# A row softmax streamed through SBUF: sixteen tiles of eight rows in six buffers become twelve tiles of eight, twelve and four rows in four buffers

## The chip, the core and the metric

The kernel runs on one NeuronCore of one Trainium2 chip. The metric is the time of one execution on the device, in microseconds (us). Five executions of the kernel before took 317.83 to 318.44 us, with a median of 317.9 us. A profile was taken of one further execution; all clock readings below are us from the first instruction of that execution.

## What is computed

The input `x` is 32 x 512 x 1024 in float32, so 16,384 rows of 1024 numbers, 67.11 MB. Each row is divided by a temperature of 0.5 and goes through a softmax.

```python
scaled = x / temperature
shifted = scaled - np.max(scaled, axis=-1, keepdims=True)
exp_x = np.exp(shifted)
return (exp_x / np.sum(exp_x, axis=-1, keepdims=True)).astype(np.float32)
```

The output is as large as the input. So 67.11 MB must be read from HBM and 67.11 MB written back; each row is read once and written once.

## The kernel before

A tile holds 128 x k rows: each of the 128 SBUF partitions holds k consecutive rows of the matrix, 4 KiB each. Below, "rows" always means rows per partition, so the whole job is 128 rows and one row is 128 x 4 KiB = 0.524 MB. `TILES` (L10) lists the tiles: sixteen of eight rows. Loads, arithmetic and stores all use the same buffer; `BUFS` (L11) says how many buffers there are, six of 32 KiB per partition.

`load` (L57 to L62) takes the next tile of the list and issues its load on the SP queue (L61). In DRAM, the eight rows of one partition lie side by side (`dram`, L50 to L53), so a tile is moved as 128 contiguous pieces of 32 KiB. A load into a buffer that was used before waits until the store out of that buffer has landed.

The arithmetic runs over groups of `GROUP` = 4 rows (L13, list built in L39 to L48), so a tile of eight rows has two groups. For a group g there are four steps:

- `maximum` (L64): VectorE (DVE) finds the row maxima, one TENSOR_REDUCE over 128 x 4096 numbers (L70), and multiplies them by -2 to a bias (L73). The first group of a tile needs the whole tile to have landed, as the load is one DMA.
- `exponential` (L75): ScalarE (ACT) runs one ACTIVATE for each row (L79), which also adds up the row's sum.
- `divide` (L88): DVE takes the reciprocal of the sums (L91) and multiplies each row by it (L93).
- `store` (L97): after the last group of a tile, the store of the whole tile is issued on the ACT queue (L101), and then `load` is called, which gives SP the load that reuses this buffer.

The order on every engine is the program order, since the body runs under a manual schedule (L107). The loop at L110 interleaves neighbouring groups: for each g it issues `maximum(g)` and `exponential(g)`, and after them `divide(g - 1)` and `store(g - 1)`. So DVE works on the maxima of group g while ACT still has the exponentials of g - 1. It also means that the store of a tile comes after the first `maximum` of the next tile, which waits for the next tile's load.

Of the kernel before, what the change touches and what calls it, by code (L numbers as in the profile page):

```python
# [1 line left out]

# [4 lines left out]

TILES = [[8]] * 16  # L10
BUFS = 6  # L11

GROUP = 4  # L13


@with_exitstack
def kernel(
    ctx: ExitStack,
    tc: tile.TileContext,
    x: bass.AP,  # L20
    temperature: bass.AP,
    out: bass.AP,
):
    nc = tc.nc
    f32 = mybir.dt.float32
    scale = 1.0 / float(temperature)
    extreme = mybir.AluOpType.max if scale > 0 else mybir.AluOpType.min

    P = 128
    xf = x.flatten_outer_dims()  # L30
    of = out.flatten_outer_dims()
    n, d = xf.shape
    assert sum(sum(ks) for ks in TILES) * P == n

    data = ctx.enter_context(tc.tile_pool(name="data", bufs=BUFS))
    stats = ctx.enter_context(tc.tile_pool(name="stats", bufs=4))


    groups, first, r = [], [], 0  # L39
    for i, ks in enumerate(TILES):  # L40
        first.append(r)
        r += sum(ks)
        a = 0
        for k in ks:
            for b in range(0, k, GROUP):
                m = min(GROUP, k - b)
                groups.append((i, a + b, m, (a, k) if b + m == k else None))
            a += k  # L48

    def dram(t, i):  # L50
        k = sum(TILES[i])
        block = t[P * first[i] : P * (first[i] + k), :]
        return block.rearrange("(p k) d -> p k d", p=P, k=k)  # L53

    tiles, small = [], []

    def load():  # L57
        i = len(tiles)
        if i < len(TILES):
            xt = data.tile([P, sum(TILES[i]), d], f32, name="xt")  # L60
            nc.sync.dma_start(out=xt, in_=dram(xf, i))  # L61
            tiles.append(xt)  # L62

    def maximum(g):  # L64
        i, a, k, _ = groups[g]
        top, bias, sums, recip = (
            stats.tile([P, k], f32, name=name) for name in ("top", "bias", "sums", "recip")
        )
        small.append((bias, sums, recip))
        nc.vector.tensor_reduce(  # L70
            out=top, in_=tiles[i][:, a : a + k, :], axis=mybir.AxisListType.X, op=extreme
        )
        nc.vector.tensor_scalar_mul(bias, in0=top, scalar1=-scale)  # L73

    def exponential(g):  # L75
        i, a, k, _ = groups[g]
        bias, sums, _ = small[g]
        for b in range(k):
            nc.scalar.activation(  # L79
                tiles[i][:, a + b, :],  # L80
                tiles[i][:, a + b, :],
                mybir.ActivationFunctionType.Exp,
                bias=bias[:, b : b + 1],
                scale=scale,
                accum_out=sums[:, b : b + 1],
            )

    def divide(g):  # L88
        i, a, k, _ = groups[g]
        _, sums, recip = small[g]  # L90
        nc.vector.reciprocal(recip, sums)  # L91
        for b in range(k):
            nc.vector.tensor_scalar_mul(  # L93
                tiles[i][:, a + b, :], in0=tiles[i][:, a + b, :], scalar1=recip[:, b : b + 1]
            )

    def store(g):  # L97
        i, _, _, part = groups[g]
        if part:
            a, k = part  # L100
            nc.scalar.dma_start(out=dram(of, i)[:, a : a + k, :], in_=tiles[i][:, a : a + k, :])  # L101
            if a + k == sum(TILES[i]):
                load()

    with tc.manual_schedule():  # L107
        for _ in range(BUFS):
            load()
        for g in range(len(groups) + 1):  # L110
            if g < len(groups):
                maximum(g)
                exponential(g)
            if g > 0:
                divide(g - 1)
                store(g - 1)


# [1 line left out]
_INS = ['x', 'temperature']  # L120
_OUTS = [((32, 512, 1024), 'float32')]

_NUMBERS = {'temperature': 0.5}


# [26 lines left out]
```

## Time and profile before

| What | Value |
|---|---|
| median of five executions | 317.9 us |
| the profiled execution: its own time | 317.9 us |
| the profiled execution: span from first to last instruction | 316.0 us |
| time around the span (the difference) | 1.9 us |
| DVE busy | 235.5 us, 75% of the span |
| ACT busy | 149.6 us, 47% of the span |
| bytes moved by the 16 DMA engines | 134.25 MB, 425 GB/s over the span |
| loads: number, size, median from issue to landing | 16, 4096 KB, 50.2 us |
| stores: number, size, median from issue to landing | 16, 4096 KB, 38.7 us |

How to read the views used below. The page cuts the span into 40 slices; a digit is the busy share of a slice in tenths, for DMA the mean over the core's 16 DMA engines. For a DMA queue, the page gives its packets, the MB it moved, and the time that its packets took as a share of the span of all 16 engines. q1 carries the loads from SP, q10 the stores from ACT, q14 fetches instructions. The same view can be asked for any stretch of the span; there a packet counts with its whole duration in the stretch in which it starts, so that a short stretch can show more than 100%. A row of the groups gives line, engine, operation, shapes and count, then the busy time in us and the mean ns of one, then the engine's idle time ahead of it and what ended most of it.

### The profile page before, as it was taken

The numbers are of one execution on the slowest core, as the hardware profiler recorded it, in microseconds if no ns is written. First come the engines' busy times: TensorE is split into PE (matmuls) and PEld (weight loads), VectorE is DVE, ScalarE is ACT, GpSimd is POOL, SyncE is SP. The second block draws the span as 40 slices with busy tenths as digits, with TensorE's granted clock in tenths as the row PEclk, the third lists the DMA queues.
The fourth block names the chain that finished last, engine by engine and source line by source line (L and its number), as shares of the span: only waits on it lengthen the run. The fifth ranks groups of instructions, "written<-read, shape, count | busy, mean of one in ns | idle before, by whom it ended". The sixth has DMA issues, their size and how long they took to land.

```text
span 316.0 us, 620 instructions
## 1 busy us (share of the span) xinstructions
DVE 235.5 (75%) x224; ACT 149.6 (47%) x257; POOL 0.2 (0%) x4
## 2 busy tenths in 40 slices
DVE  0399999999689494994949859498693976949720
ACT  0176666666526255361554605546064560645500
POOL 0000000000000000000000000000000000000000
DMA  8999999999999999999999999999999999999996
GB/s 332 406 456 419 377 460 402 460 417 444 423 440 435 431 440 427 448 415 448 415 452 411 452 407 456 411 456 415 448 423 441 435 427 440 423 448 415 452 411 274
DMA packets 4612, 134.25 MB, mean 425 GB/s; under 512 B 512, under 2 KB 512, under 8 KB 512
## 3 DMA queue, kind: packets, MB, share of 16 engines
q1 hardware_dynamic: 2304, 67.11, 49.7%
q10 hardware_dynamic: 2304, 67.11, 49.2%
q14 instruction: 4, 0.03, 0.0%
HBM read 67.11 MB, written 67.11 MB: 425 GB/s over the span
## 4 chain that ended last, share of the span: by engine, by line
DVE 49%; DMA 32%; another core or an unknown queue 9%; ACT 5%; issue 1%; DVEq 0%; SPq 0%
DVE top L70 29%; DMA xt<-in_x_dram 20%; DVE xt L93 18%; DMA out_dram<-xt 12%; ACT xt L79 5%; DVE recip L91 1%; DVE bias L73 1%; DVEq L147 0%; SPq L61 0%
## 5 line engine op out<-in xcount | busy, mean ns | idle before, releaser
L79 ACT ACTIVATE xt<-xt,bias 128x1024 f32<-128x1024 f32 x128 | 145.4, 1137 | 136.9 <-DVE recip L91 119.5
L70 DVE TENSOR_REDUCE top<-xt 128x4 f32<-128x4096 f32 x32 | 141.3, 4416 | 62.6 <-DMA xt<-in_x_dram 62.6
L93 DVE TENSOR_SCALAR xt<-xt,recip 128x1024 f32<-128x1024 f32 x128 | 87.7, 749 | 1.1
L79 ACT ACTIVATION_READ_ACCUMULATOR xt<-xt,bias 128x1 f32 x128 | 23.8, 186 | 0.0
L79 ACT ACT_TABLE_LOAD x1 | 1.3, 1283 | 13.0 <-DMA xt<-in_x_dram 13.0
L91 DVE RECIPROCAL recip<-sums 128x4 f32<-128x4 f32 x32 | 5.5, 171 | 2.1 <-ACT xt L79 2.1
L73 DVE TENSOR_SCALAR bias<-top 128x4 f32<-128x4 f32 x32 | 5.4, 170 | 1.1
L133 POOL MEMSET const-uint8-127<- 128x1 uint8 x1 | 0.1, 102 | 0.0
L133 POOL MEMSET const-bfloat16-1.0<- 128x1 bf16 x1 | 0.1, 101 | 0.0
L133 POOL MEMSET const-float32-0.0<- 128x1 f32 x1 | 0.1, 98 | 0.2 <-issue 0.2
L133 POOL MEMSET const-float32-1.0<- 128x1 f32 x1 | 0.1, 98 | 0.0
## 6 DMA issues: line engine op xcount, KB each, us to landing
xt<-in_x_dram SPq DMA_DIRECT2D x16, 4096.0 KB, 50.2
out_dram<-xt ACTq DMA_DIRECT2D x16, 4096.0 KB, 38.7
```

The lines of the kernel that those rows point to most:

```text
L70: nc.vector.tensor_reduce(out=top, in_=tiles[i][:, a : a + k, :], axis=mybir.AxisListType.X, op=extreme)
L73: nc.vector.tensor_scalar_mul(bias, in0=top, scalar1=-scale)
L79: nc.scalar.activation(tiles[i][:, a + b, :], tiles[i][:, a + b, :], mybir.ActivationFunctionType.Exp, bias=bias[:, b : b + 1], scale=scal ...
L91: nc.vector.reciprocal(recip, sums)
L93: nc.vector.tensor_scalar_mul(tiles[i][:, a + b, :], in0=tiles[i][:, a + b, :], scalar1=recip[:, b : b + 1])
L133: nc = _bacc.Bacc("TRN2", target_bir_lowering=False, num_devices=1)
```

## The change

The list of tiles becomes one tile of eight rows, nine of twelve, one of eight and one of four: twelve tiles, again 128 rows. There are four buffers, each as large as the largest tile, 48 KiB per partition; four times 48 KiB is the 192 KiB that six times 32 KiB were. A twelve-row tile has three groups, so there are 32 groups as before, and the instructions on DVE and ACT are the same in kind and number. There are 24 DMAs where there were 32.

The loop gets a second order. `alone` is true where group g is the first of a new tile and the tile of g - 1 is the tenth of the list or a later one (index 9 or 10 of 0 to 11). This is so at two places: between the last twelve-row tile and the eight-row tile, and between the eight-row tile and the four-row tile. There, `divide(g - 1)` and `store(g - 1)` come ahead of `maximum(g)` and `exponential(g)` and not after them.

```diff
-TILES = [[8]] * 16
-BUFS = 6
+TILES = [[8]] + [[12]] * 9 + [[8], [4]]
+BUFS = 4
...
         for g in range(len(groups) + 1):
+
+            alone = 0 < g < len(groups) and groups[g][0] > groups[g - 1][0] >= len(TILES) - 3
+            if alone:
+                divide(g - 1)
+                store(g - 1)
             if g < len(groups):
                 maximum(g)
                 exponential(g)
-            if g > 0:
+            if g > 0 and not alone:
                 divide(g - 1)
                 store(g - 1)
```

## The prediction

> **What bounds the kernel now.** I first read slices and queues on the page: is one resource full from end to end?
>
> ```profile
> DMA  8999999999999999999999999999999999999996
> q1 hardware_dynamic: 2304, 67.11, 49.7%
> q10 hardware_dynamic: 2304, 67.11, 49.2%
> ```
>
> The DMA engines are: 98.9% of 316.0 us is 312.5 us of packets, and only the first and the last slice show a hole. Next, whether the engines are also waited for. The waits of all engines say:
>
> ```profile
> ACT xt L79 <- DVE recip L91: 119.5, 25, 7.9
> DVE top L70 <- DMA xt<-in_x_dram: 62.6, 12, 12.9
> ```
>
> DVE sits 62.6 us waiting for loads, so the chain of waits, which puts 49% of the span on DVE, only follows it from load to load. Third, the pace of the full stretch, in the DMA view of 40 to 280:
>
> ```profile
> DMA packets 3557, 103.84 MB, mean 433 GB/s; under 512 B 385, under 2 KB 385, under 8 KB 385
> q1 hardware_dynamic: 1777, 51.91, 50.1%
> q10 hardware_dynamic: 1776, 51.91, 50.1%
> ```
>
> Both queues always have work and share equally. One row (0.524 MB) costs 0.524 / 433 = 1.211 us of all engines, 2.42 us while the two queues share. The kernel ends when 256 row-moves are through, unless at some moment both queues are empty. So the change can gain only in packets, in the start or in the end, and lose only where it makes a hole.
>
> **Packets: the one thing removed.** 4608 data-queue packets less the page's 512 small ones leave 4096 of 32 KiB: 32 DMAs of 128 pieces, 256 for each engine. After: nine tiles x 8 pieces x 2 directions = 144 of 48 KiB, 32 of 32 KiB and 16 of 16 KiB, together 192. 64 fewer; their fixed part is gained. It comes from two sizes. A 32 KiB packet takes 50.1% x 16 x 240 / (51.91 MB / 32 KiB = 1584) = 1.2146 us. Two 8 KB instruction fetches stand in the DMA view of 65.02 to 65.38:
>
> ```profile
> q14 instruction: 2, 0.02, 10.7%
> ```
>
> 10.7% x 16 x 0.36 / 2 = 0.308 us each. Fixed part: (4 x 0.308 - 1.2146) / 3 = 5.8 ns, from 4 to 8 ns with the rounding. 64 x 5.8 ns = **0.37 us gained** (0.24 to 0.54). This is an estimate: a fetch does not end in SBUF, and no packet over 32 KiB was seen. Bounds for the longer packet: none of the gain (0), or it is cut up on the way, 0.5 to 1.3 us lost (below). I take 0.37, as the two sizes seen lie on that side. The 8 small packets fewer on each engine I count at nothing.
>
> The Trainium skill (DMA: Bandwidth & Descriptors, Where 436 GB/s comes from) puts the ceiling at 435.2 GB/s. The row says 433; at the ceiling the 134.2 MB would take 308.4 us for 310.0, so by the page no longer packet could gain more than 1.6 us.
>
> **The start.** Tile 0 is still eight rows, issued first and landed at 12.9: nothing moves. The hole it contains is the latency of the first load, unchanged. There is one loss where the first store joins the loads; q1 in the DMA views of 33.8 to 35.0 and of 35.0 to 37:
>
> ```profile
> q1 hardware_dynamic: 16, 0.52, 130.3%
> ```
> ```profile
> q1 hardware_dynamic: 16, 0.52, 85.3%
> ```
>
> 16 packets, one per engine: 1.303 x 1.2 = 1.56 us and 0.853 x 2.0 = 1.71 us, for 1.21. So 0.35 + 0.49 = 0.84 us is lost once. After, the first store is still a 32 KiB one, among 48 KiB loads. Bounds: all of it saved (-0.84), or half as much again (+0.42). I take no change, since the event is the same.
>
> **The middle: fewer, larger buffers.** The load into a buffer waits for the store out of it, so I check whether the loads run dry. Before: the first store is issued at 32.6, and q10 first moves at 37.2 (no q10 packet in the view of 35.0 to 37), 4.6 us later. By then 8 + (37.2 - 12.9 - 0.84) / 1.211 = 27.4 rows are loaded; this lead stays, as the queues share equally. It foretells the page's medians. After load k+1 lands, store k is issued 7.4 us later (next maximum and divide) and is through (27.4 - 8) x 2.42 = 46.9 us after that landing: 39.5 from issue, the page has 38.7. The load that reuses the buffer lands 5 x 19.37 - 46.9 = 50.0 later; the page has 50.2. Of these 50 us only 19.4 are its own transfer, the rest is waiting in the queue.
>
> After: tile 1 (20 rows in) lands at 12.9 + 12 x 1.211 = 27.4, store 0 is issued at 34.8 and moves at 39.4; the lead is 8 + (39.4 - 12.9 - 0.84) / 1.211 = 29.2 rows. A twelve-row tile takes 29.1 us in each queue. Store k is through (29.2 - 12) x 2.42 = 41.7 us after load k+1 lands; the next load has 3 x 29.1 - 41.7 = 45.5 us, of which it needs 29.1. 16 us remain to spare (31 before). DVE needs 3 x 7.39 = 22.2 us of 29.1. So **no hole, nothing gained or lost**. Were this cover gone, the stores would run alone at the full pace and still no engine would be idle.
>
> **The end: new order, smaller tiles.** Before (timeline, engine line op, start first):
>
> ```profile
> 282.65 4.42 DVE L70 TENSOR_REDUCE top<-xt 128x4 f32<-128x4096 f32 x1 [4.49 <-DMA xt<-in_x_dram]
> ...
> 299.43 0.18 DVE L91 RECIPROCAL recip<-sums 128x4 f32<-128x4 f32 x1 [1.91 <-ACT xt L79]
> 299.64 2.74 DVE L93 TENSOR_SCALAR xt<-xt,recip 128x1024 f32<-128x1024 f32 x4
> 302.42 0.34 ACTq L101 DMA_DIRECT2D out_dram<-xt  x1
> ```
>
> The last load lands at 282.6; 32.6 us of stores remain until the last lands (302.42 + 12.8 = 315.2), and the engines stay full. So the end does not wait for arithmetic now, and a shorter last tile has no wait to remove. It must only keep up. By the lead, loads would end at 37.2 + (128 - 27.4) x 2.42 = 280.9 before (it was 282.6, so I add 1.7) and at 39.4 + 98.8 x 2.42 + 1.7 = 280.4 after; tile 10 lands 9.7 earlier at 270.7, tile 9 at 251.3. SP issues loads 10 and 11 after stores 6 and 7, whose 80 and 92 rows are out at 234.8 and 263.8, in time.
>
> Each step: maximum and bias 4.6, exponentials of a group 4.65, reciprocal and multiply 2.95. Tile 9: three interleaved groups 22.2; then, as its last divide now stands alone, 1.7 of waiting for ACT and 2.95: store 9 at 278.2. It's due when store 8 is out (104 rows, 285.0). Tile 10: 4.6 + 4.4 + 2.95, then 1.9 of waiting and 2.95: store 10 at 295.0, due at 299.5. Tile 11: 4.6 + 4.65 + 2.95: store 11 at 307.2. The two orders written out cost DVE about 3.6 us of waiting that interleaving would hide, beside which the stores of tiles 9 and 10 run; nothing else is queued behind those waits but the next maximum on DVE and its exponentials on ACT. In exchange store 9 passes 4.6 us of maximum, and store 10 no longer waits for load 11. Due time of store 11: the end without a hole is 315.2 - 0.4 = 314.8; its own four rows take 4.8, and before, the last store spent 12.8 - 9.7 = 3.1 us on issue, queue and landing: 306.9. The sum lands on the edge. Without the 1.7 I added it is 1.4 us early, with it 0.3 late; I take **0**, and each us that tile 9 lands later costs one.
>
> A rule that speaks against the small last tile: equal shares by bytes are what the row above shows, for equal packets. The Trainium skill (DMA: Bandwidth & Descriptors, Queues, rings and completion order) says that an engine takes turns between queues by packets, so a load in 16 KiB packets beside stores in 48 KiB ones would get a quarter. By that, load 10 would land some 5 us and load 11 some 14 us later than in my sum, about 276 and 294, still ahead of the DVE times at which they are needed (278 and 295). No run here has shown unequal packets.
>
> **Sum.** 316.0 - 0.37 + 0 = 315.6 us of span, and 1.9 around it: **317.5 us**. The profiled execution's own time is the median, 317.9, so nothing is added. That's 0.1% faster; about 0.2% (0.64 us) is what a measurement of this kernel can tell from no change.
>
> **Rivals.**
>
> - The first-store loss goes as well: 317.5 - 0.8 = 316.7. For it: it falls on two packets per engine only, and other packets are then in flight. Against: the joining store is unchanged.
> - The end runs dry (slower). Place: between stores 10 and 11, DVE being the chain. Point: tile 9 landing after 251. Price: one for one; 2 us later gives 319.5. For it: the sum has no margin. Against: 1.7 of it was added on top of the lead.
> - The pieces are not moved whole: cut in two (24 KiB) an engine has 288 + 32 + 16 = 336 packets, 80 more, +0.5 instead of -0.4: 318.4; cut into 16 KiB, 480, +1.3: 319.2. The change would then not do what it says. Against: 32 KiB pieces move whole. I set 318.8.
>
> **Chances.** Forecast 0.58, with its own range 316.9 to 318.3; first-store loss gone 0.13; end dry 0.14; pieces cut or paced worse 0.15. Faster by over 0.2% (under 317.3): 0.13 and about a quarter of the forecast's 0.58, 0.27. Slower by over 0.2% (above 318.5): 0.14 and two thirds of 0.15, 0.24. Within: 0.49. Range 316.6 to 319.5: it takes in most of the first and third rivals and half of the second.
>
> **What would show it.** Queues with 1728 packets each (24 DMAs for both: 1536 + 192 each), DMA 9 in every slice but first and last, 433 to 435 GB/s in the full stretch, loads about 45 us from issue to landing, last store issued near 305 to 307 with stores full up to it. It's wrong if a slice between 280 and 312 shows a hole, if packets are more, or if the pace falls.

## The result, and the profile after

The changed kernel takes 318.63 us (median of 28 executions, 318.18 to 320.61) against 317.95 us of the kernel before (48 executions): ratio 1.0033, 95% interval 1.0024 to 1.0041. It's **slower by 0.7 us**, where 0.4 us faster was forecast. The time lies in the forecast range (316.6 to 319.5), but the sign is the other one. A second series of the same kernel (e12 below) gave 1.0017 (1.0007 to 1.0027), so the size is 0.2 to 0.3%. The executions of the changed kernel scatter more: 18 of 28 lie from 318.2 to 318.9, six from 320.2 to 320.7. The profiled execution took 318.2 us, 316.4 of them its span, so it is one of the shortest.

Slices and queues on the page of the changed kernel, as they were read for before:

```profile
DMA  8999999999999999999999999999999999999995
...
q1 hardware_dynamic: 1728, 67.11, 49.6%
q10 hardware_dynamic: 1728, 67.11, 49.1%
```

The packets are as many as foretold, 1728 in each queue, and no slice but the first and the last has a hole (a stretch in which engines are idle). The share, 98.7% of 316.4, is 312.3 us of packets (312.5 before). So there is neither more DMA work nor a hole, and still the end is later. The DMA view of 40 to 280 has the old pace; only the shares differ:

```profile
DMA packets 2527, 104.02 MB, mean 433 GB/s; under 512 B 272, under 2 KB 272, under 8 KB 272
q10 hardware_dynamic: 1264, 53.74, 51.7%
q1 hardware_dynamic: 1259, 50.25, 48.5%
```

The arithmetic is not late either. The end in the timeline, as shown for before:

```profile
290.20 4.42 DVE L70 TENSOR_REDUCE top<-xt 128x4 f32<-128x4096 f32 x1
...
299.58 0.18 DVE L91 RECIPROCAL recip<-sums 128x4 f32<-128x4 f32 x1 [4.75 <-ACT xt L79]
299.79 2.74 DVE L93 TENSOR_SCALAR xt<-xt,recip 128x1024 f32<-128x1024 f32 x4
302.56 0.34 ACTq L101 DMA_DIRECT2D out_dram<-xt  x1
```

The last store is issued at 302.56, as before (302.42), though it carries half as much.

What did move is seen only when the 16 DMA engines are counted one by one. Every DMA ends on every engine with one small packet (the page of the changed kernel has 384 for its 24 DMAs); in the last stretch, "under 512 B" is therefore the number of engines that have finished. The DMA views of 312.6 to 313.05, 313.05 to 314.2 and 314.2 to 316.5, first of before:

```profile
DMA packets 1, 0.03 MB, mean 73 GB/s; under 512 B 0, under 2 KB 0, under 8 KB 0
DMA packets 16, 0.07 MB, mean 57 GB/s; under 512 B 14, under 2 KB 14, under 8 KB 14
DMA packets 2, 0.00 MB, mean 0 GB/s; under 512 B 2, under 2 KB 2, under 8 KB 2
```

and of the changed kernel:

```profile
DMA packets 15, 0.10 MB, mean 219 GB/s; under 512 B 9, under 2 KB 9, under 8 KB 9
DMA packets 11, 0.13 MB, mean 114 GB/s; under 512 B 3, under 2 KB 3, under 8 KB 3
DMA packets 7, 0.05 MB, mean 21 GB/s; under 512 B 4, under 2 KB 4, under 8 KB 4
```

By 313.05 nine engines are done where none was: the first ends at 312.70 for 313.09, by the records of the closing packets, which is the gain that was worked out. But four engines, for two, end after 314.2, the last at 315.24 for 314.83. The kernel waits for the last one. From the first engine's end to the last one's it is 1.74 us before and 2.54 us in the changed kernel.

Single packets show what makes an engine late. A window that holds the start of one packet gives its duration, share x 16 x width. DMA views of the changed kernel at 235.8 to 235.9, 236.1 to 236.15, 188.88 to 188.92 and 281.3 to 281.5:

```profile
q14 instruction: 1, 0.01, 19.3%
```
```profile
q1 hardware_dynamic: 1, 0.05, 294.1%
```
```profile
q1 hardware_dynamic: 1, 0.05, 355.0%
```
```profile
q10 hardware_dynamic: 1, 0.05, 77.1%
```

The first is an instruction fetch of 0.31 us; the second the 48 KiB packet behind it, 2.35 us where others take 1.815. One fetch holds one engine back by 0.31 + 0.54 us. The kernel before has these too, four fetches in each trace. The records don't name the engine, but on one engine a packet starts as the one ahead of it ends, so it can be followed from packet to packet. Before, the four fetches fall on two engines, two on each, and these two end last, at 314.49 and 314.83, 1.40 and 1.74 us behind the first; fetches and excess behind them add up to 1.37 and 1.69 us. So it is the fetches that make these two late.

The third (2.27 us) and the fourth (2.47 us) have no fetch near them. The third starts where the load queue has just gone over to its next tile, the fourth beside the 16 KiB packets of the last load. I call a packet slow that takes over 60 ns more than its size needs. After 40 us, before has 4 slow packets, all behind fetches, 1.8 us of excess in all; the changed kernel has 23, 6.5 us in all. Of the 19 behind no fetch, 12 start where a queue has just gone over to its next tile, and all but one fall on the five engines that end last. The very last had no fetch at all.

### The profile page after: what moved, and what is told of

The parts are those of the page before. It is cut to its first block, busy times and chain, and to the rows that moved or that the text cites. A ratio compares the mean times of both kernels' runs of the same rounds, so it can differ in the third digit from the quotient of the medians.

```text
span 316.4 us, 605 instructions
## 1 busy us (share of the span) xinstructions
DVE 235.5 (74%) x224; ACT 149.5 (47%) x257; POOL 0.2 (0%) x4
## 3 DMA queue, kind: packets, MB, share of 16 engines
q1 hardware_dynamic: 1728, 67.11, 49.6%
q10 hardware_dynamic: 1728, 67.11, 49.1%
## 4 chain that ended last, share of the span: by engine, by line
DMA 77%; DVE 12%; ACT 5%; issue 1%; DVEq 0%; SPq 0%; ACTq 0%
DMA xt<-in_x_dram 40%; DMA out_dram<-xt 38%; DVE top L70 8%; ACT xt L79 5%; DVE xt L93 3%; DVE bias L73 0%; DVEq L152 0%; DVE recip L91 0%; SPq L61 0%; ACTq L79 0%
## 6 DMA issues: line engine op xcount, KB each, us to landing
xt<-in_x_dram SPq DMA_DIRECT2D x9, 6144.0 KB, 36.7
out_dram<-xt ACTq DMA_DIRECT2D x9, 6144.0 KB, 42.6
```

## The experiments

Each ratio is to the kernel before, run beside it. "Ends" are first and last closing packet of the last store, from the records of the trace.

**e1: the end interleaved again.**

```diff
-            alone = 0 < g < len(groups) and groups[g][0] > groups[g - 1][0] >= len(TILES) - 3
+            alone = False
```

> The changed kernel with the second order taken out: the last two tiles are interleaved like all others; tiles and buffers stay as changed. Theory (the 48 KiB pieces let the 16 DMA engines drift apart, and the last engine sets the end; in the trace of the changed kernel the stores never run dry): time as the changed kernel, 318.6 us within 0.3, ratio to before 1.002 to 1.004. Rival (the end written out alone costs time): back to 317.9.

Measured 319.83 us (318.74 to 320.6, six runs), ratio 1.0054 (1.0035 to 1.0073). Both expectations missed: it is slower than the changed kernel. So nothing is gained by leaving the new order out, and it is needed: store 10 now waits for load 11 (landed at 291.4) and is issued at 298.9 for 290.2, and a hole opens. Its stretch of 296 to 300; the last columns are DMA share and GB/s:

```profile
296.00:300.00 4.00, 2.83 (x6) 3.91 (x7) 0.00 (x0) 1.00 0.79 340
```

**e2: the twelve-row tiles moved by two DMAs**, of eight and four rows, loads and stores alike.

```diff
+    def pieces(i):
+        k = sum(TILES[i])
+        return [(lo, min(lo + 8, k)) for lo in range(0, k, 8)]
...
-            nc.sync.dma_start(out=xt, in_=dram(xf, i))
+            for lo, hi in pieces(i):
+                nc.sync.dma_start(out=xt[:, lo:hi, :], in_=dram(xf, i)[:, lo:hi, :])
```

> The changed kernel, same tiles, buffers and order, but each twelve-row tile is moved by two DMAs, of eight and of four rows, so that no packet is over 32 KiB. 336 data packets per engine for 192. Theory of the long pieces: the spread of the engines at the end goes back to that of before, 317.9 us and some 0.5 for 80 more packets than before at 5.8 ns: 318.0 to 318.5, and none of the runs near 320. Rival (tile list or four buffers spread the engines, not the size of a packet): 318.6 + 144 x 5.8 ns = 319.4.

Measured 318.66 us (318.48 to 319.23, ten runs), ratio 1.002 (1.0011 to 1.0028). Between the two: above the theory's 318.5, well under the rival's 319.4. No run came near 320. 13 slow packets, 4.3 us, in a profiled execution that was the longest of the ten (319.23). Undecided by itself: the number of DMAs changed with the length, and a fifth instruction fetch falls into the span (at 300.8).

**e3: before with four buffers of 32 KiB** (`BUFS = 4`).

> The kernel before with four buffers of 32 KiB in place of six; nothing else. Theory of the long pieces: no change, 317.9 within 0.3, as the loads still have work queued or the stores run alone at full pace. Rival (fewer buffers cost time by themselves): 318.5 or more, and a hole in some slice of the DMA row.

Measured 323.97 us, ratio 1.0187 (1.0174 to 1.0201). The theory's expectation failed; by the packets' own times each engine is idle for some 4 us from 293 to 299, and for 2.5 us from 308 to 311. Its stretches of 292 to 296 and 296 to 300:

```profile
292.00:296.00 4.00, 3.93 (x5) 1.00 (x1) 0.00 (x0) 1.00 0.46 197
296.00:300.00 4.00, 4.00 (x4) 3.64 (x8) 0.00 (x0) 1.00 0.60 254
```

With 128 KiB of buffers for 192 the loads run dry once, early (the fourth lands at 48.9, the fifth is issued at 52.8), so they end late (last landing at 290.3, before 282.6), and the last two tiles are then not ready when the stores have drained. The changed kernel has 192 KiB and no hole. The trace has 25 slow packets, all of 32 KiB, and 21 of them are behind no fetch: a slow packet doesn't need 48 KiB.

**e4: the changed end alone**, on 32 KiB packets and six buffers.

```diff
-TILES = [[8]] + [[12]] * 9 + [[8], [4]]
-BUFS = 4
+TILES = [[8]] * 15 + [[4], [4]]
+BUFS = 6
```

> The kernel before with six buffers of 32 KiB and fifteen tiles of eight rows, then two of four, the last tiles not interleaved: the change's end without its long pieces. Theory of the long pieces: 317.9 within 0.3 (16 packets more per engine are 0.1). Rival (the end written out alone and the small last tile cost the time): 318.5 or more.

Measured 318.35 us (eleven runs), ratio 1.0012 (1.0004 to 1.0021): 0.3 to 0.4 us, between the two expectations. Its trace (318.83, the second longest) has a small hole, a DMA share of 0.69 from 308 to 310, since the last store is issued only at 308.2. So written-out orders can cost where the chain at the end has no room; in the changed kernel there was room (302.56).

**e5: blocks of their own.** As e2, but the eight-row and the four-row part are contiguous blocks in DRAM.

```diff
-    def dram(t, i):
-        k = sum(TILES[i])
-        block = t[P * first[i] : P * (first[i] + k), :]
+    def dram(t, i, lo, hi):
+        k = hi - lo
+        block = t[P * (first[i] + lo) : P * (first[i] + hi), :]
```

> As e2 (changed tiles and buffers, two DMAs for a twelve-row tile, no packet over 32 KiB), but the two parts are blocks of their own in DRAM, of 128 x 8 and 128 x 4 contiguous rows, so that the pieces of neighbouring partitions lie 32 and 16 KiB apart and not 48. So far: in the changed kernel 23 packets after 40 us took over 60 ns too long, 6.5 us in all, most of them where one of the queues passes to its next tile, and the last engine ended 1.8 us after the mean one; before it was 4 packets, 1.8 us in all, and 1.3 us. Theory now (layout: a pitch of 48 KiB makes lagging engines collide at the change of tile): 318.0 to 318.4, clearly under e2's 318.66, hardly any slow packet at a change of tile. Rival (four large buffers: little work queued in front of each engine): as e2, 318.5 to 318.8.

Measured 318.71 us (eleven runs), ratio 1.0021 (1.0012 to 1.003): as e2, which is where the rival had it. The layout theory falls. Here too a fifth fetch is in the span (299.2).

**e6: before with pieces 96 KiB apart.**

```diff
+        j, c = divmod(i, 3)
+        block = t[P * 24 * j : P * 24 * (j + 1), :].rearrange("(p k) d -> p k d", p=P, k=24)
+        return block[:, 8 * c : 8 * c + 8, :]
```

> The kernel before (sixteen tiles of eight rows, six buffers, 32 KiB packets) with another assignment of rows: three tiles share a block of 24 rows per partition, so that the pieces lie 96 KiB apart; the last tile as before. Theory of the layout: 318.3 to 319, with slow packets at changes of tile. Rival (buffers): 317.9 to 318.1, unchanged.

Measured 317.95 us, ratio 1.0 (0.9992 to 1.0009), the same 4 slow packets behind the four fetches. The layout theory falls a second time.

**e7: before with more instructions.**

```diff
         nc.vector.reciprocal(recip, sums)
+        if g < len(groups) - 4:
+            for _ in range(8):
+                nc.vector.memset(spare, 0.0)
```

> The kernel before with 224 additional tiny DVE instructions (eight memsets of 128x1 per group, none in the last four groups), so that about two more 8 KB instruction fetches fall into the span. In both traces each fetch (0.31 us) and the packet behind it (0.25 to 0.55 us more) hold one engine back by 0.6 to 0.85 us. Theory that the last engine sets the end, and that what holds single engines back is what counts: up to 0.8 us more where a fetch falls on the engine that is already last, so 317.9 to 319, spread of the engines' ends larger. Rival (a late engine costs nothing, as the queues make up for it): 317.9, unchanged.

Measured 319.85 us (six runs), ratio 1.0064 (1.0048 to 1.008). This is above the theory's 319 and far from the rival's 317.9. The profile fell on the longest of the six (321.45; the others took 319.7 to 320.0). It has six fetches for four, and 23 slow packets, 17 of them behind no fetch. The DMA views of 314.2 to 315 and 315 to 319:

```profile
DMA packets 16, 0.03 MB, mean 41 GB/s; under 512 B 15, under 2 KB 15, under 8 KB 15
DMA packets 3, 0.07 MB, mean 16 GB/s; under 512 B 1, under 2 KB 1, under 8 KB 1
```

Fifteen engines are done by 315; one comes at 318.3, 3.6 us behind. Followed from packet to packet, it's the one on which four of the six fetches fall (44.5, 118.1, 194.1 and 300.7). Part of the loss is a hole of 0.8 us per engine, since the last load is complete only when the late engine has its part (284.2, before 282.6). The edit also adds 13 us to DVE, so that e7 alone does not settle whether fetches or DVE do it; e14 does.

**e8: ten rows in five buffers.**

```diff
-TILES = [[8]] + [[12]] * 9 + [[8], [4]]
-BUFS = 4
+TILES = [[8]] + [[10]] * 11 + [[6], [4]]
+BUFS = 5
```

> The changed kernel with tiles of ten rows in five buffers of 40 KiB (8, eleven of 10, 6, 4), the same order at the end. Packets of 40 KiB lie 40 KiB apart. Theory of the layout: 318.4 or more, as the pitch is odd and the packets are long. Rival (too few buffers): nearer to before, 317.6 to 318.2.

Seven of twelve runs took 318.5 to 318.8 us, five took 340 to 344. The ratio, 1.0021 (1.0011 to 1.0031), is that of the seven; the profile fell among the others (span 342.4). In it 156 packets are slow, 73 us in all, and a tile lands up to 36 us later on the last engine than on the first. Why five executions went so is not known. Packets of 40 KiB are no better than those of 48: the seven took what the changed kernel takes. The layout theory had foretold 318.4 or more, but e5 and e6 speak against it.

**e9: before with five buffers** (`BUFS = 5`).

> The kernel before with five buffers of 32 KiB in place of six. By the lead of 27 rows the next load has 4 x 19.4 - 46.9 = 31 us until it is due and needs 19.4, so that 11 us of it is waiting in the queue (31 before, 16 in the changed kernel), and no store is late. Theory (long packets make engines that are behind fall further behind): as before, 317.8 to 318.2, few slow packets. Rival (a short queue of loads in front of the engines does it, whatever the packet): 318.4 or more, with slow packets where a queue passes to its next tile, as in the changed kernel.

Measured 317.95 us, ratio 0.9995 (0.9987 to 1.0004), 4 slow packets. Its loads took 31.4 us (page, median), so 12 us of that is waiting in the queue, and the rival falls for a queue of that length. In the changed kernel the wait turned out as 7.6 us and not 16 (below), and in e3, with its many slow packets, it is 7.2 (26.6 less 19.4). So a shorter queue than that of e9 isn't ruled out.

**e10: before in packets of 16 KiB.** A gap in the SBUF tile cuts the pieces; DMAs and order stay.

```diff
-            xt = data.tile([P, sum(TILES[i]), d], f32, name="xt")
-            nc.sync.dma_start(out=xt, in_=dram(xf, i))
+            xt = data.tile([P, 2, GROUP * d + 8], f32, name="xt")
+            nc.sync.dma_start(out=xt[:, :, : GROUP * d], in_=halves(dram(xf, i)))
```

> The kernel before with a gap of 32 B after each four rows in the SBUF tile, so that every load and store goes in 16 KiB packets; number of DMAs, tiles, buffers and order as before. 512 data packets per engine for 256. Packets of 16, 32 and 48 KiB took 611, 1213 and 1815 ns in the trace of the changed kernel, which is a fixed part of 9 ns; 5.8 ns were predicted. Expected by either theory: 256 x 5.8 to 9 ns more, 1.5 to 2.3 us, so 319.4 to 320.3; and a spread of the engines' ends as before (1.7 us) or less.

Measured 319.41 us (319.29 to 319.58), ratio 1.0041 (1.0029 to 1.0053). 1.3 us for 256 packets more, 5.1 ns each, a little under the expected 1.5.

**e11: the changed kernel with more instructions**, the edit of e7.

> The changed kernel with 224 additional tiny DVE instructions, as in e7, where they brought two more instruction fetches and cost the kernel before 1.9 us. Theory that an engine held back falls further behind, and more so with 48 KiB packets: 2 to 4 us over the changed kernel, 320.5 to 322.5. Rival (each hold costs its 0.6 to 0.85 us and no more): under 1.7, up to 320.3.

Measured 320.6 us (319.56 to 322.77), ratio 1.0081 (1.0056 to 1.0106), 2.0 us over the changed kernel. No hole; ends 313.3 and 317.6, two engines after 314.2. The theory's lower edge, but the interval of 0.8 us to each side takes in the rival's 1.7, and e7 lost 1.9 with 32 KiB packets: that a held engine falls further behind with 48 KiB ones isn't shown by it.

**e12: the changed kernel again.**

> The changed kernel once more, for a second trace and for its times: 318.2 to 318.9 in most runs and near 320.4 in about a third. Theory (the last engine sets the end): in the trace, the time of the first engines to end is 312.7 within 0.3, and whatever the run is longer than 316.2 is the lateness of a few engines, without a hole in the others. Rival (a hole opens at the end in the long runs): all engines end late together.

Measured 318.48 us (318.26 to 319.96, eleven runs), ratio 1.0017 (1.0007 to 1.0027). Its trace repeats the first: 16 slow packets, 4.1 us, no hole, ends 312.75 and 315.64. The DMA views of 312.6 to 313.05, 313.05 to 314.2 and 314.2 to 316.5:

```profile
DMA packets 15, 0.05 MB, mean 109 GB/s; under 512 B 12, under 2 KB 12, under 8 KB 12
DMA packets 6, 0.07 MB, mean 57 GB/s; under 512 B 2, under 2 KB 2, under 8 KB 2
DMA packets 5, 0.05 MB, mean 21 GB/s; under 512 B 2, under 2 KB 2, under 8 KB 2
```

Fourteen engines are early by the gain, two are late. One run of eleven, not a third, came near 320; no profile fell on such a run, so what those are stays open.

**e13: the changed kernel in packets of 16 KiB**, by the gap of e10. Tiles, buffers, DMAs, order and bytes in front of the engines are those of the changed kernel.

```diff
+            xt = data.tile([P, sum(TILES[i]) // GROUP, GROUP * d + 8], f32, name="xt")
+            nc.sync.dma_start(out=xt[:, :, : GROUP * d], in_=parts(dram(xf, i)))
```

> The changed kernel with a gap of 32 B after each four rows in the SBUF tile, as e10 did it with the kernel before: tiles, buffers, DMAs and order as changed, every packet 16 KiB, 512 per engine as in e10. Theory (the 48 KiB packet is what holds engines back at the change of tile): as e10, 319.2 to 319.7, and hardly a slow packet but those behind the instruction fetches. Rival (twelve-row tiles in four buffers or the unequal list do it): slow packets at the changes of tile again, and about as much over e10 as the changed kernel's lateness is, 0.5 to 2 us, so 320 or more.

Measured 319.34 us (319.18 to 319.46), ratio 1.004 (1.0026 to 1.0054): e10's time. Its loads on the page:

```profile
q1 hardware_dynamic: 4288, 67.11, 49.7%
```

That is 4096 packets of 16 KiB and 192 small ones. After the first store has joined (41.2 us), the four packets behind the fetches are the only slow ones, and the ends are 1.86 us apart (e10: 1.91). So with packets of 16 KiB the twelve-row tiles, the four buffers and the new end cost nothing that shows (the intervals leave some 0.4 us), and **the packets of the changed kernel are the cause**. Which property of theirs is not separated, as e13 makes them shorter and all equal at once. In the changed kernel, 2.8 of the 4.8 us of excess behind no fetch (in e12 1.7 of 2.4) fall after 246, where stores of 48 KiB run beside loads of 32 and 16 KiB; the rest falls where both queues move 48 KiB.

**e14: before with fewer instructions**, in the first twelve tiles.

```diff
         nc.vector.reciprocal(recip, sums)
+        if i < 12:
+            nc.vector.tensor_tensor(
+                out=tiles[i][:, a : a + k, :],
+                in0=tiles[i][:, a : a + k, :],
+                in1=recip.unsqueeze(2).to_broadcast([P, k, d]),
+                op=mybir.AluOpType.mult,
+            )
+            return
```

> The kernel before with 72 DVE instructions fewer: in the first twelve tiles the four multiplications of a group are one TENSOR_TENSOR with the reciprocals broadcast along the row. DVE's second instruction fetch (at 240 us in the trace of before, when 168 of its 224 instructions had run) should fall away; it held one engine back by 0.8 us. Theory (what holds single engines back sets the end): 0 to 0.8 us less, 317.1 to 317.9, the spread of the engines' ends smaller. Rival (the fetches cost the end nothing, e7's loss came from its DVE time): no change or, as DVE gets longer, slower.

Measured 317.37 us (317.26 to 317.55, eleven runs), ratio 0.9984 (0.9975 to 0.9993): **faster than both kernels**, though DVE works 40 us more. The new row of the groups, and the DMA view of 312.6 to 314.2:

```profile
L93 DVE TENSOR_TENSOR xt<-xt,recip 128x4096 f32<-128x4096 f32 x24 | 106.2, 4425 | 0.8
```
```profile
DMA packets 18, 0.07 MB, mean 41 GB/s; under 512 B 16, under 2 KB 16, under 8 KB 16
```

A group's multiplication takes 4.43 us where four rows took 2.74, all beside the transfers. Three fetches are in the span for four, and all 16 engines end from 312.98 to 314.03. The two engines that take the fetches are still the last, but 0.9 and 1.05 us behind the first, where before they were 1.40 and 1.74. The rival, for which a longer DVE could only cost, falls.

**e15: the changed kernel with fewer instructions**, the same edit in its first nine tiles (`if i < 9`).

> The changed kernel with the same edit in its first nine tiles, 60 DVE instructions fewer and over 20 us more on DVE. Theory: the lateness of the last engines goes down, 317.3 to 318.4, under the changed kernel's 318.5 to 318.6. Rival: no gain, 318.5 or more.

Measured 318.29 us (eleven runs), ratio 1.0014 (1.0005 to 1.0023): the theory's side, but e12's ratio of 1.0017 lies within this interval, so that a gain isn't shown. Its trace, of the shortest execution (317.94), has 32 slow packets and five engines after 314.2: with one fetch less, the packets of the changed kernel still spread the engines.

## Why the prediction was wrong

- **What bounds the kernel**: right that DMA does, and that neither DVE nor ACT matters. The step that failed is the sentence that the kernel ends when 256 row-moves are through unless both queues are empty, and the one built on it, that the change can lose only where it makes a hole. That treats 16 engines as one. Each engine has its own share of the packets, and the end is the last engine's. The sum had no term for lateness, and the trace of before already had it: ends from 313.09 to 314.83. The change took the first end 0.39 us forward and the last 0.41 us back (e12: 0.34 and 0.81).
- **Packets**: the mechanism and the size hold. 5.8 ns each was worked out; e10 gives 5.1, so 64 packets are 0.33 us, and the first engines ended 0.39 (e12: 0.34) earlier. What failed is the bounds: no gain or cut up. The longer packet had a price of another kind, slow packets on engines that are behind: about 1 us at the median (0.7 measured loss and 0.33 gain given away). It falls neither under a cut nor under a slower pace: the pace is 433 GB/s in both. That the time lies in the range all the same is luck, as the range reached so far up for a dry end and for cut pieces, and neither came.
- **The start**: right. The first store costs once as much as before. The DMA view of the changed kernel, 37 to 38.3:

```profile
q1 hardware_dynamic: 16, 0.79, 207.5%
```

  2.075 x 1.3 = 2.70 us for 1.815, so 0.88 us per engine; 0.84 was taken over from before. The first rival falls.
- **The middle**: no hole, as said. But the loads landed 36.7 us after issue and not 45.5, so 7.6 us were to spare and not 16. The lead was mis-sized: equal shares were assumed while the first store, in 32 KiB packets, ran beside 48 KiB loads. The DMA view of 43 to 62 there:

```profile
q1 hardware_dynamic: 112, 4.72, 57.4%
q10 hardware_dynamic: 112, 3.67, 44.7%
```

  The longer packet gets the larger share: while 8 rows were stored, loads gained some 3 to 4 rows. A lead of 29.2 rows becomes 32.8, and (32.8 - 12) x 2.42 = 50.3 us fits 7.4 + 42.6, the stores' measured time from issue. The remark that with the cover gone no engine would be idle was wrong: in e3 none is idle while the loads are dry, but the loads end later for it, and the holes at the end cost 6 us.
- **The end**: no hole, as said, but not on the edge. Store 11 was issued at 302.56 and not 307.2, since by that lead tile 9 landed at 246 and not 251. The rival of a dry end falls for this kernel; e1 shows it where the second order is left out. The unequal shares are here too: load 11, in 16 KiB packets, landed 19.6 us after load 10, in e13 with equal packets 14.6. So it came at 290.18 and not at 280.4, just as DVE was free for it (290.20 above). Eight turns of a 16 KiB and a 48 KiB packet (0.611 and 1.815 us) are 19.4 us. This agrees with the turns by packets that the Trainium skill states (DMA: Bandwidth & Descriptors, Queues, rings and completion order), with the difference that the page's typical packet is many descriptors and here the turns go by single pieces. The DMA view of 275 to 283 has the loads at 29%, near the quarter that the prediction worked out:

```profile
q10 hardware_dynamic: 59, 2.41, 71.4%
q1 hardware_dynamic: 61, 1.00, 29.1%
```

- **Pieces not moved whole**: falls; 1728 packets in each queue.

Not settled: why a packet on an engine that is behind stalls where a queue passes to its next tile. The layout (e5, e6) is ruled out as the cause; that it lies in the packets is shown (e13), the mechanism is not. Three things that may take part were not tested apart: the length, the unequal lengths in the two queues, and a short queue of loads (some 7 us of waiting in e3 and in the changed kernel, 10 in e13, 12 in e9). e2 and e5 lie 0.25 us over what their 80 packets cost (0.4), with 12 or 13 slow packets and a fifth fetch each; this too is open.

## What to carry to other kernels

Where DMA is full from end to end, count the engines one by one at the end: the mean share can be the same while the last engine decides. A longer packet saves 5 ns each and can cost more than that in engines that drift apart; past 32 KiB per partition it wasn't worth it here. An instruction stream has a price beyond its engine's time, since each 8 KB fetch holds one DMA engine back by 0.6 to 0.85 us, and here the holds added up on the same two engines: fewer, larger instructions made this kernel faster although they took longer.

## What the runs showed of the hardware that was not expected

- An instruction fetch of 0.31 us costs the engine it falls on 0.27 to 0.54 us more in the packet behind it (the kernel before and the changed one).
- The fetches keep to two DMA engines: two on each in the kernel before and in the changed one, four and two with more DVE instructions (e7), one and two with fewer (e14). In before, e7 and e14 the engine that they hold back most ends last.
- With 40 KiB packets (e8) five of twelve executions took 21 us or more longer than the others, and in the trace of one of them the engines were up to 36 us apart; the cause is open.
- Unequal packets gave the two queues unequal shares while both had work: 57% to 45% for 48 against 32 KiB.
